# High and low activation parts interleaved by element in the gate stage of an encoder

## The chip, the cores and the metric

The kernel runs on one core of a Trainium2 chip. The metric is the time of one execution on the device, in microseconds (us). The engines are TensorE (PE in the profile; PEld is its loading of the stationary operand), VectorE (DVE), ScalarE (ACT), GpSimd (POOL) and SyncE (SP), which here only issues DMAs.

## What is computed

The reference is an encoder of two layers over 512 tokens of width 1024, batch 1, all in float32. Each layer adds a feed-forward, a mixer of four kinds of attention, a second feed-forward, and at its end a gated input:

```
for i in range(DEPTH):                      # DEPTH = 2
    x = x + 0.5 * swiglu(rms_norm(x, ffn1_norm[i]), ...)
    ...                                     # four attentions on x @ w_in, then w_out
    x = x + 0.5 * swiglu(rms_norm(x, ffn2_norm[i]), ...)
    gate = jax.nn.sigmoid(rms_norm(x, ple_norm[i]) @ ple_w_gate[i])
    x = x + gate * (p[i] @ ple_w_proj[i])
return rms_norm(x, final_norm)
```

Here `p[i]` is 512 x 256, `ple_w_proj[i]` 256 x 1024 and `ple_w_gate[i]` 1024 x 1024. The last two lines of the loop are the stage that the change touches; it is called the gate stage below.

## The kernel before

Activations lie transposed: a tile has 128 features on the partitions and the 512 tokens along the free dimension, and x is eight such tiles (`self.x`). [...] For an activation, `split` (L115) writes both into one tile of 128 x 2 x 512 words: ScalarE copies the source (with the gain of the norm as scale, L122, or without, L119) into `hl[:, 0]`, which rounds it, and VectorE writes the rest, source minus high part, into `hl[:, 1]` (L123 or L120). The 512 high words lie in a row and the 512 low words behind them. Weights come by DMA as float32 (`pieces`, L150) and are split the same way into `wh` (L173, ScalarE) and `wl` (L175, VectorE, or GpSimd in the mixer), a few pieces ahead of their use.

A product of a weight block and an activation tile is three matmuls into one PSUM tile, in `mm3y` (L195): high weight by high activation (L200), high by low (L201), low by high (L202). The weight block is the stationary operand (128 x 128), the activation part the moving one (128 x 512).

The orders of TensorE and of the DMA queue of SyncE are those of the program (`manual_schedule` in `run`, L846); the other engines are ordered by the framework's planner, and waits follow from which tiles an instruction reads and writes.

The gate stage goes so. While the second feed-forward writes its last results, `ple_in` (L827) loads the two tiles of p and splits them into `keep` tiles (`self.pin`). As each of the eight tiles of x is finished (L316, L317), `feed` (L251) splits x times the gain of the coming norm into a tile from `act()`, appended to `self.xn`, and `squared` adds to the sum of squares. `self.norm` holds the layer and the offset of that gain; G_PLE stands for the norm of the gate stage. `ple` (L793) then loops over 8 output tiles m: 6 matmuls for the projection of p (`pp`, with `pin`) and 24 for the gate (`gp`, with the eight tiles `xs`). At m = 0 the sum of squares is reduced (`rstat`, L221) and during m = 1 spread to all partitions (`rspread`, L239). `ple_out` (L818) scales the gate, takes a tanh, multiplies by `pp`, adds to x, and feeds the next stage. Two tags, "act" and "big", swap their roles after each layer (`self.tags.reverse()`), so in the rows the split tiles of x in the gate stage are named act in layer 0 and big in layer 1, and those of p keep. After layer 1 `final` (L837) scales the plain tiles that `feed` made in its other branch (L261) and stores them.

Of the kernel before, what the change touches and what calls it, by code (L numbers as in the profile page):

```python
# [29 lines left out]
G_FFN1, G_MIX, G_FFN2, G_PLE, G_GRP, G_Q, G_KV = 0, 8, 16, 24, 32, 40, 42  # L30
# [4 lines left out]
class Encoder:  # L35
# [215 lines left out]
    def feed(self, m, square=True):  # L251
        nc = self.nc
        l, off = self.norm
        t = self.act()
        if l < self.depth:
            self.split(t, self.x[m], self.g(l, off, m))
        else:
            self.squared(m)
            square = False
            t = t[:, 0].bitcast(F32)  # L260
            nc.scalar.activation(t, self.x[m], AF.Copy, scale=self.g(l, 0, m))  # L261
        self.xn.append(t)
        if square:
            self.squared(m)
# [562 lines left out]
    def ple_in(self, l):  # L827
        nc, a = self.nc, self.a
        self.pin = []
        for k in range(2):  # L830
            t = self.tmp()
            nc.sync.dma_start(t, a["p"][l, :, k])
            s = self.keep()
            self.split(s, t)
            self.pin.append(s)

# [8 lines left out]
    def run(self):  # L845
        with self.tc.manual_schedule(engines={mybir.EngineType.PE, mybir.EngineType.SP}):  # L846
            self.setup()
            self.begin(0, G_FFN1)
            for m in range(KC):
                self.feed(m, False)  # L850
                if m == 3:
                    self.prep()
            for l in range(self.depth):
                self.ffn(l, 0, (l, G_MIX))
                self.mix(l, (l, G_FFN2))
                self.ffn(l, 1, (l, G_PLE))
                self.ple(l, (l + 1, G_FFN1))
            self.final()


def grid(t, blocked=False):
# [118 lines left out]
```

## Time and profile before

| | us |
|---|---|
| Time before, median of 2 runs | 2167.8 |
| lowest and highest | 2166.63, 2168.96 |
| Span of the profiled execution | 2163.3 |
| TensorE matmuls busy in it | 2117.2 |
| VectorE busy | 1210.5 |
| ScalarE busy | 930.1 |
| GpSimd busy | 280.0 |

The profiled execution is one run, from its first instruction to its last. Its matmuls are pipelined: each is given as 0.39 us long, and the next one starts before it ends, so the pace of the stream is read from the starts, not from the lengths.

### The profile page before, as it was taken

Reading aid. Unit: us, or ns where it says so; the run is one execution under the profiler, and the core shown is the slowest. Engines: PE = TensorE matmul, PEld = TensorE weight load, DVE = VectorE, ACT = ScalarE, POOL = GpSimd, SP = SyncE. Lnnn points to the kernel's source line nnn. Section 1 sums busy time; section 2 is a strip of 40 time slices with the busy share of each in tenths; the row PEclk is TensorE's granted clock in tenths of the full one; section 3 lists DMA queues with packets and bytes.
Section 4 is the critical chain, followed back from the end, with each engine's and each line's share of the span. In section 5 each row is a group of like instructions: output and inputs, shape, how many; then the busy total and the mean of one; then the engine's idle time right before and its main releaser. Section 6 shows DMA issues by size and latency. Waiting matters only on the chain.

```text
span 2163.3 us, 25721 instructions
## 1 busy us (share of the span) xinstructions
PE 2117.2 (98%) x9564; PEld 1718.6 (79%) x9564; DVE 1210.5 (56%) x1926; ACT 930.1 (43%) x1690; POOL 280.0 (13%) x230
## 2 busy tenths in 40 slices
PE   8999999999999999999999999999999999999997
PEld 6888888677778888888888888886777788888886
DVE  5444446567766444456654444555687654444554
ACT  4332334477754332333533233345677533233343
POOL 2000001444321000001100000025332200000011
PEclk9999999999999999999999999999999999999998
DMA  3232223212112222223322322232121122322322
GB/s 129 97 109 99 98 94 111 90 60 75 40 54 93 98 96 99 98 98 96 100 96 98 94 102 98 93 102 93 64 59 49 59 98 98 94 101 98 102 92 89
DMA packets 63358, 195.38 MB, mean 90 GB/s; under 512 B 7552, under 2 KB 15872, under 8 KB 63232
## 3 DMA queue, kind: packets, MB, share of 16 engines
q1 hardware_dynamic: 61808, 187.92, 26.0%
q0 software_dynamic: 1280, 5.77, 1.0%
q8 instruction: 75, 1.23, 0.2%
q14 instruction: 51, 0.42, 0.1%
q10 hardware_dynamic: 144, 0.05, 0.0%
HBM read 189.51 MB, written 2.10 MB: 89 GB/s over the span
## 4 chain that ended last, share of the span: by engine, by line
PE 92%; DVE 4%; ACT 2%; issue 1%; DMA 1%; POOL 0%; POOLq 0%; SPq 0%; DVEq 0%; ACTq 0%
PE ps L200 15%; PE ps L201 15%; PE ps L202 15%; PE s L201 13%; PE s L200 13%; PE s L202 13%; PE pv L455 2%; PE s L439 2%; PE s L398 2%; PE s L397 1%; DVE kl L343 1%; PE s L225 1%; PE s L236 0%; ACT tmp L326 0%; DVE PT L443 0%
## 5 line engine op out<-in xcount | busy, mean ns | idle before, releaser
L173 ACT ACTIVATE wh<-raw 128x512 fp32r<-128x512 f32 (+1 forms) x712 | 437.8, 615 | 971.2 <-PE ps L201 457.3
L175 DVE TENSOR_TENSOR wl<-raw,wh 128x512 fp32r<-128x512 f32 (+1 forms) x614 | 435.6, 710 | 405.6 <-ACT wh L173 399.0
L200 PE MATMUL ps<-act,wh 128*128 128x512 f32 x616 | 248.8, 404 | 6.1 <-ACT act L122 6.1
L216 POOL TENSOR_TENSOR acc<-acc,tmp 128x512 f32<-128x512 f32 x54 | 72.3, 1340 | 1365.4 <-ACT tmp L215 1365.0
L200 PE MATMUL ps<-big,wh 128*128 128x512 f32 x616 | 247.0, 401 | 0.0
L201 PE MATMUL ps<-act,wh 128*128 128x512 f32 x616 | 242.7, 394 | 3.3 <-DVE act L123 3.1
L202 PE MATMUL ps<-act,wl 128*128 128x512 f32 x616 | 242.1, 393 | 0.0
L202 PE MATMUL ps<-big,wl 128*128 128x512 f32 x616 | 240.6, 391 | 0.0
L201 PE MATMUL ps<-big,wh 128*128 128x512 f32 x616 | 240.3, 390 | 0.0
L200 PE MATMUL s<-act,wh 128*128 128x512 f32 x520 | 202.4, 389 | 0.0
L200 PE MATMUL s<-big,wh 128*128 128x512 f32 x520 | 202.4, 389 | 0.0
L202 PE MATMUL s<-act,wl 128*128 128x512 f32 x520 | 202.3, 389 | 0.0
L202 PE MATMUL s<-big,wl 128*128 128x512 f32 x520 | 202.3, 389 | 0.0
L201 PE MATMUL s<-big,wh 128*128 128x512 f32 x520 | 202.3, 389 | 0.0
L201 PE MATMUL s<-act,wh 128*128 128x512 f32 x520 | 202.3, 389 | 0.0
L175 POOL TENSOR_TENSOR wl<-raw,wh 128x512 fp32r<-128x512 f32 (+1 forms) x98 | 127.4, 1300 | 286.6 <-ACT wh L173 286.4
L200 PEld LDWEIGHTS ps<-act,wh 128*128 128x128 f32 x616 | 116.7, 189 | 30.1 <-ACT act L122 6.4
L201 PEld LDWEIGHTS ps<-act,wh 128*128 128x128 f32 x616 | 116.7, 189 | 28.5 <-DVE act L123 7.3
L202 PEld LDWEIGHTS ps<-act,wl 128*128 128x128 f32 x616 | 116.6, 189 | 24.6
L202 PEld LDWEIGHTS ps<-big,wl 128*128 128x128 f32 x616 | 115.7, 188 | 24.7
L200 PEld LDWEIGHTS ps<-big,wh 128*128 128x128 f32 x616 | 116.0, 188 | 23.5 <-issue 1.1
L201 PEld LDWEIGHTS ps<-big,wh 128*128 128x128 f32 x616 | 116.2, 189 | 21.4
(172 smaller groups left out, 3373.1 us busy)
## 6 DMA issues: line engine op xcount, KB each, us to landing
raw<-in_ffn_gu SPq DMA_DIRECT2D x175, 512.0 KB, 3.5
raw<-in_ffn_d SPq DMA_DIRECT2D x64, 512.0 KB, 3.4
raw<-in_w_in SPq DMA_DIRECT2D x40, 512.0 KB, 3.5
raw<-in_ffn_d SPq DMA_DIRECT2D x64, 192.0 KB, 2.5
raw<-in_w_out SPq DMA_DIRECT2D x16, 512.0 KB, 3.5
raw<-in_ple SPq DMA_DIRECT2D x16, 384.0 KB, 3.0
raw<-in_ple SPq DMA_DIRECT2D x16, 256.0 KB, 2.6
nb<-in_na_bias POOLq DMA_DIRECT2D x8, 448.0 KB, 4.1
```

What stands on the lines that cost most here:

```text
L173: nc.scalar.activation(hi, r, AF.Copy)
L175: eng.tensor_tensor(out=lo, in0=r, in1=hi.bitcast(F32), op=ALU.subtract)
L200: nc.tensor.matmul(ps, lhsT=wh[:, k], rhs=x[:, 0], start=start and k == 0, stop=False)
L201: nc.tensor.matmul(ps, lhsT=wh[:, k], rhs=x[:, 1], start=False, stop=False)
L202: nc.tensor.matmul(ps, lhsT=wl[:, k], rhs=x[:, 0], start=False, stop=stop and k == last)
L216: eng.tensor_tensor(out=acc, in0=acc, in1=sq, op=ALU.add)
L225: nc.tensor.matmul(ss[:, t:t + 1], lhsT=acc[:, t * 128:(t + 1) * 128], rhs=self.ones, start=True, stop=True)
L343: nc.vector.tensor_tensor(out=kl[r], in0=u[r], in1=t[r, e].bitcast(F32), op=ALU.subtract)
L397: nc.tensor.matmul(s, lhsT=q[:, e, qs], rhs=k[0][:, e, k0:k1], start=True, stop=False)
L398: nc.tensor.matmul(s, lhsT=q[rows, e, qs], rhs=k[1][rows, k0:k1], start=False, stop=True)
L439: nc.tensor.transpose(tp[:, t * 128:(t + 1) * 128], h["P"][t][:, o:o + 128], self.ident)
L455: nc.tensor.matmul(pv[:, c], lhsT=vb, rhs=h["pt"][b][:, i, c], start=b == 0 and i == 0, stop=b == 3 and i == 1, skip_group_check=True)
```

## The change

The tiles that the gate stage's matmuls read as moving operands keep their size of 2 x 512 words for a partition, but are addressed so that high and low part of one element lie side by side: word 2t is the high part of token t, and word 2t + 1 its low part. `hl[:, 0]`, `hl[:, 1]`, `x[:, 0]` and `x[:, 1]` then stand for every second word. This holds for the eight tiles of the normed x of that stage (in `feed`, where the offset is that of its norm) and for the two tiles of p (in `ple_in`), in both layers. All other tiles, the weights, the instructions and their order in the program are as before.

```diff
@@ def feed @@
         t = self.act()
+        if off == G_PLE:
+            t = pairs(t)
         if l < self.depth:
             self.split(t, self.x[m], self.g(l, off, m))
@@ def ple_in @@
-            s = self.keep()
+            s = pairs(self.keep())
             self.split(s, t)
             self.pin.append(s)
@@ new function @@
+def pairs(t):
+    return t.rearrange("p a t -> p (a t)").rearrange("p (t a) -> p a t", a=2)
```

## Rows read from the trace of the kernel before

**Rows 1.** Head of the page: span, and busy time, share and instructions of each engine.
```profile
span 2163.3 us, 25721 instructions
PE 2117.2 (98%) x9564; PEld 1718.6 (79%) x9564; DVE 1210.5 (56%) x1926; ACT 930.1 (43%) x1690; POOL 280.0 (13%) x230
```

**Rows 2.** Page: the chain that ended last, share of the span by engine.
```profile
PE 92%; DVE 4%; ACT 2%; issue 1%; DMA 1%; POOL 0%; POOLq 0%; SPq 0%; DVEq 0%; ACTq 0%
```

**Rows 3.** Waits of TensorE, longest in total first: total us, times, longest us.
```profile
PE ps L200 <- ACT act L122: 6.1, 1, 6.1
PE s L368 <- DVE tmp L361: 6.0, 2, 3.0
PE s L397 <- DVE ne L404: 4.7, 4, 1.4
```

**Rows 4.** Windows over the gate stages of layers 0 and 1, busy us by engine.
```profile
core 0: us, PE busy (x) PEld busy (x) DVE busy (x) ACT busy (x) POOL busy (x), PEclk, DMA share, GB/s
1024.84:1080.66 55.82, 55.82 (x254) 46.33 (x252) 38.52 (x57) 27.64 (x48) 8.80 (x7) 1.00 0.32 97
2090.20:2145.86 55.66, 55.66 (x252) 45.98 (x251) 29.49 (x48) 26.23 (x46) 8.77 (x7) 1.00 0.26 78
```

**Rows 5.** Timeline of TensorE, gate stage of layer 0: start us, us, instruction.
```profile
1024.84 0.39 PE L200 MATMUL ps<-keep,wh 128*128 128x512 f32 x1
...
1026.20 0.39 PE L200 MATMUL s<-act,wh 128*128 128x512 f32 x1
...
1030.96 0.39 PE L200 MATMUL s<-act,wh 128*128 128x512 f32 x1
...
1080.66 0.39 PE L200 MATMUL ps<-big,wh 128*128 128x512 f32 x1
```

**Rows 6.** Timeline of TensorE, among the first matmuls of the kernel.
```profile
7.44 0.63 PE L202 MATMUL ps<-act,wl 128*128 128x512 f32 x1
7.87 0.63 PE L200 MATMUL ps<-act,wh 128*128 128x512 f32 x1
...
9.05 0.63 PE L202 MATMUL ps<-act,wl 128*128 128x512 f32 x1
9.47 0.62 PE L200 MATMUL ps<-act,wh 128*128 128x512 f32 x1
10.15 0.50 PE L201 MATMUL ps<-act,wh 128*128 128x512 f32 x1
```

**Rows 7.** Timelines of ScalarE and VectorE: split of the eighth tile, layers 0 and 1.
```profile
1026.83 0.73 ACT L122 ACTIVATE act<-x,gain 128x512 fp32r<-128x512 f32 x1 [1.43 <-DVE x L317]
1027.59 0.75 DVE L123 SCALAR_TENSOR_TENSOR act<-x,gain,act 128x512 fp32r<-128x512 f32 x1 [0.80 <-ACT act L122]
2092.79 0.75 DVE L123 SCALAR_TENSOR_TENSOR big<-x,gain,big 128x512 fp32r<-128x512 f32 x1 [0.80 <-ACT big L122]
```

**Rows 8.** Line 123 on VectorE: ns least/median/most, first and last start.
```profile
L123 DVE SCALAR_TENSOR_TENSOR act<-x,gain,act x32: 736/752/1832, 6.0 to 1027.6; 128x512 fp32r<-128x512 f32 x32
L123 DVE SCALAR_TENSOR_TENSOR big<-x,gain,big x32: 739/751/1835, 1044.3 to 2092.8; 128x512 fp32r<-128x512 f32 x32
```

**Rows 9.** Timeline of TensorE, first and last matmul of layer 1's gate stage.
```profile
2090.03 0.39 PE L200 MATMUL ps<-keep,wh 128*128 128x512 f32 x1
...
2145.63 0.39 PE L202 MATMUL s<-big,wl 128*128 128x512 f32 x1
```

**Rows 10.** Timelines: DMAs of p in layer 0, splits of p in layer 1.
```profile
953.23 0.86 SPq L832 DMA_DIRECT2D tmp<-in_p  x2
...
2031.78 1.90 DVE L120 TENSOR_TENSOR keep<-tmp,keep 128x512 fp32r<-128x512 f32 x3 [0.23 <-ACT keep L119]
```

## The prediction

> **What bounds the kernel now.** I read the head of the page first. The span is 2163.3 us, and TensorE's matmuls are busy for 2117.2 us of it, while VectorE has 56% and ScalarE 43% [rows 1]. A busy share of a pipelined engine proves little by itself, so the chain that ended last comes next: 92% of it is TensorE [rows 2]. Then the waits of TensorE: the longest is 6.1 us, at the start of the kernel, and the next is 6.0 us in two pieces [rows 3]. So the kernel is one stream of matmuls with hardly a hole, and a change counts by what it does to the spacing of matmuls.
>
> The change touches the gate stage that ends each layer. The stage of layer 0 lasts from 1024.84 to 1080.66 us, that of layer 1 from 2090.20 (a fifth of a microsecond after its first matmul) to 2145.86 us; TensorE is busy for all of both at a granted clock of 1.00, VectorE for 38.5 and 29.5 us and ScalarE for 27.6 and 26.2 us of some 55.7 [rows 4]. Spacing is read from starts, since the 0.39 us that one matmul lasts overlaps with the next: 21 matmuls lie between the starts 1026.20 and 1030.96, so 4.76 / 21 = 0.2267 us for 512 columns [rows 5]. [...]
>
> **The change, part by part.**
>
> *Matmuls with a step of two.* Each of the 8 output tiles takes 10 products (2 of the projection of p, 8 of the gate) of 3 matmuls: 30 x 8 = 240 in a layer, 480 in both. 240 x 0.2267 = 54.4 us, which is the stage but for its norm and transposes [rows 4, 5]. All 480 lie on the path that sets the end, one after another. The count stays the same; only the read of the moving operand changes, from 512 words in a row to every second of 1024. No row of this trace has a matmul, or any other instruction, that reads or writes with a step of two words, so the price is bounded:
> [...]
> - Nothing: the read has room to spare.
> - Twice the spacing: each fetch brings neighbouring words, and half of each is thrown away. Doubling 0.2267 gives +0.2267 x 480 = 108.8 us. The nearest rows with a spacing of about that size are the first matmuls of the kernel, 0.43 us (7.44 to 7.87) and 0.42 us (9.05 to 9.47) [rows 6]; they are slow for another reason than a step, but they are the same instruction shape. By 0.42 us the term is (0.42 - 0.2267) x 480 = 92.8 us.
> - Far end: the longest spacing in those rows is 0.68 us (9.47 to 10.15) [rows 6], +0.453 x 480 = 217.6 us.
>
> I take the doubled case, at the middle of its bounds: +0.21 us a matmul, 480 x 0.21 = 100.8 us. The reason is a comparison of rates: TensorE takes a word per partition every 0.2267 / 512 = 0.44 ns [rows 5], ScalarE's pass over 512 words lasts 0.73 us and VectorE's 0.75 us [rows 7], 1.4 and 1.5 ns a word. [...] If the memory hands out neighbouring words together, TensorE is the engine that lives on it. This is a choice and not a reading.
>
> [...]
>
> *Splits that write with a step of two.* In each layer 8 tiles of the normed x (ScalarE writes the high part, VectorE reads it and writes the low part) and 2 tiles of p: 20 pairs of instructions in all. Below, they cost what they cost now. Above, from the slowest row of that instruction, VectorE's goes from 0.75 to 1.83 us [rows 8], and ScalarE's doubles, from 0.73 to 1.46: 20 x 1.08 = 22 us and 20 x 0.73 = 15 us of busy time, beside engines that idle for 17 us or more of each stage [rows 4] and a matmul stream that would only be longer. The latest is the eighth tile of x: its low part ends at 1027.59 + 0.75 = 1028.34 [rows 7], and the first matmul on the tile starts at 1030.96 [rows 5], 2.6 us of cover; in layer 1 it is 2093.54 against 2096.15 (2090.03 + 27 x 0.2267) [rows 7, 9]. The upper bounds add 1.08 + 0.73 = 1.8 us, within it; without that cover each layer would pay what goes beyond 2.6 us. The tiles of p are issued at 953.23 for a first read at 1024.84, and split by 2033.68 for 2090.03 [rows 5, 9, 10]. I cost all this at nothing.
>
> *A wait that moves.* High and low parts now interleave, so their address ranges overlap. If dependencies go by ranges, the high matmul also waits for the low part. Queued behind it on TensorE is the whole stream, but the times just given are those of the low part, so the 2.6 us cover this too: nothing.
>
> *After the stage.* The next feed-forward's tiles and weights come no earlier; with TensorE slower, the others have more time. The tail after the last gate matmul (2145.63 to the span's end, 17.7 us [rows 9]) moves as a block; the last stage writes no interleaved tile for the final norm.
>
> **Sum.** 2163.3 + 100.8 = 2264.1 us of span; the median of the runs stands 4.5 us above the profiled span, so 2268.6 us.
>
> **Rivals.**
> [...]
> 2. *Partly hidden.* Fetches overlap in part, and the spacing lands half way to 0.43 us: (0.43 - 0.2267) / 2 x 480 = 48.8 us, 2217 us. [...]
> 3. *Worse than double.* The step lands on conflicts, or the clock drops as well: 0.68 us a matmul, 2168 + 218 = 2385 us. Nothing in these stages points to it: the clock is 1.00 in both [rows 4].
>
> **How the numbers follow.** Doubled 0.58, no change 0.28, partly hidden 0.09, worse 0.05. The forecast is that of the doubled case, 2268.6 us; its own range is 2258 to 2280 (92.8 to 108.8 us, and a little around it). As the rival without cost holds more than 2 in 10, the whole range reaches down to it and its gain, 2161, and up to 2285, for splits that are not wholly hidden. 2% of 2167.8 us are 43 us, about what a measurement of this kernel can tell from no change. Slower by more: the doubled and the worse case and most of the partly hidden one, 0.70. Within: the rival without cost and the rest, 0.29. Faster by 2%: 0.01, since the largest gain found is 6.4 us.
>
> **What would show it.** Right: in the timeline of the stage, starts of matmuls on interleaved tiles 0.42 to 0.45 us apart, matmuls of the other stages still at 0.227; each stage some 106 us long by the windows; VectorE and ScalarE with the same busy time in a stage nearly twice as long; no new wait of TensorE on a split. Wrong: a spacing of 0.227 in the stage (rival 1), 0.30 to 0.38 (rival 2), over 0.5 (rival 3), or a hole ahead of the first matmul on the eighth tile, which would make the splits the bound.

## The result and the profile after

The changed kernel takes 2274.2 us (two runs, 2273.68 and 2274.72) where the kernel before takes 2167.8: a ratio of 1.0489, 95% interval 1.0469 to 1.0508. The profiled execution spans 2271.9 us, 108.6 us more than before.

The head of its page and the chain that ended last, which answer to [rows 1, 2]:

```profile
span 2271.9 us, 25721 instructions
PE 2226.4 (98%) x9564; PEld 1730.5 (76%) x9564; DVE 1206.5 (53%) x1926; ACT 931.1 (41%) x1690; POOL 279.3 (12%) x230
...
PE 92%; DVE 4%; ACT 2%; issue 2%; DMA 1%; POOL 0%; SPq 0%; POOLq 0%; DVEq 0%; ACTq 0%
```

The instruction counts are the same on every engine. TensorE's busy time has grown by 109.2 us, about as much as the span; VectorE and ScalarE are where they were (1206.5 against 1210.5, 931.1 against 930.1). The shares of the chain look all but unchanged, and that is the trap of shares: nothing in them says that some matmuls became twice as slow.

The longest waits of TensorE in the changed kernel (total us, times, longest us), against [rows 3]:

```profile
PE s L370 <- DVE tmp L363: 6.0, 2, 3.0
PE ps L200 <- ACT act L122: 5.9, 1, 5.9
PE s L399 <- DVE ne L406: 4.6, 4, 1.4
```

The same three waits, each within 0.2 us of its length before (the diff moves line numbers beyond `feed` by two), and no new wait on a split among the longest. So the time is not in a hole. The windows over the two gate stages, columns as in [rows 4]:

```profile
core 0: us, PE busy (x) PEld busy (x) DVE busy (x) ACT busy (x) POOL busy (x), PEclk, DMA share, GB/s
1024.48:1134.14 109.66, 109.66 (x254) 51.91 (x252) 35.77 (x57) 28.00 (x49) 8.86 (x7) 0.98 0.18 54
2144.82:2254.46 109.64, 109.64 (x253) 51.62 (x251) 29.58 (x48) 26.65 (x46) 8.82 (x7) 0.98 0.13 40
```

The stages take 109.66 and 109.64 us, where they took 55.82 and 55.66: 107.8 of the 108.6 us are here. TensorE is busy throughout, before and after. The timeline of TensorE in the gate stage of layer 0 says how, the same four starts as in [rows 5]:

```profile
1024.48 0.61 PE L200 MATMUL ps<-keep,wh 128*128 128x512 f32 x1
...
1027.18 0.63 PE L200 MATMUL s<-act,wh 128*128 128x512 f32 x1
...
1036.69 0.63 PE L200 MATMUL s<-act,wh 128*128 128x512 f32 x1
...
1134.14 0.42 PE L200 MATMUL ps<-big,wh 128*128 128x512 f32 x1
```

21 matmuls in 9.51 us are 0.453 us each, twice the 0.2267 of before. Further on it is a little less: over the whole of both stages, without the starts next to the norm's small matmuls, the mean is 0.4515, against 0.2269 in the kernel before. 480 x (0.4515 - 0.2269) = 107.8 us, just what the two windows have grown by. The other 0.8 us of the span is not followed up; single runs of one kernel differ by more.

The split of the eighth tile, as in [rows 7]:

```profile
1026.47 0.75 ACT L122 ACTIVATE act<-x,gain 128x512 fp32r<-128x512 f32 x1 [1.44 <-DVE x L319]
1027.25 0.75 DVE L123 SCALAR_TENSOR_TENSOR act<-x,gain,act 128x512 fp32r<-128x512 f32 x1 [0.82 <-ACT act L122]
```

0.75 and 0.75 us, against 0.73 and 0.75. ScalarE's write with a step of two takes 0.02 us more, VectorE's read and write with it what they took, and the split ends 8.7 us before the first matmul on the tile (1036.69).

The granted clock of the stages is 0.98, not 1.00. In smaller windows it is one dip in each stage, shortly after the norm's single-column matmuls. Two windows of one microsecond in the dip of layer 0 (TensorE alone):

```profile
1041.00:1042.00 1.00, 1.00 (x3) 0.50 0.28 111
1042.00:1043.00 1.00, 1.00 (x3) 0.50 0.00 0
```

and the timeline of TensorE there:

```profile
1041.21 0.63 PE L202 MATMUL ps<-keep,wl 128*128 128x512 f32 x1
1041.66 0.63 PE L200 MATMUL s<-act,wh 128*128 128x512 f32 x1
1042.11 0.64 PE L201 MATMUL s<-act,wh 128*128 128x512 f32 x1
1042.57 0.64 PE L202 MATMUL s<-act,wl 128*128 128x512 f32 x1
1043.02 0.64 PE L200 MATMUL s<-act,wh 128*128 128x512 f32 x1
```

From 1041 to 1043 us the clock stands at 0.50, and the starts are 0.45 us apart, as they are at 1.00. Plain matmuls are slower there: where the kernel before has its clock at 0.50 (402 to 405 us), they start 0.43 us apart (403.45, 403.88, 404.31), against 0.2267 us at 1.00 [rows 4, 5]. The starts of the read with a step of two are as far apart at 0.50 as at 1.00, so it is not the granted clock that paces these matmuls.

### The profile page after: what moved, and what is told of

It is laid out like the page before. It is cut to its first block, busy times and chain, and to the rows that moved or that the text cites. A ratio compares the mean times of both kernels' runs of the same rounds, so it can differ in the third digit from the quotient of the medians.

```text
span 2271.9 us, 25721 instructions
## 1 busy us (share of the span) xinstructions
PE 2226.4 (98%) x9564; PEld 1730.5 (76%) x9564; DVE 1206.5 (53%) x1926; ACT 931.1 (41%) x1690; POOL 279.3 (12%) x230
## 4 chain that ended last, share of the span: by engine, by line
PE 92%; DVE 4%; ACT 2%; issue 2%; DMA 1%; POOL 0%; SPq 0%; POOLq 0%; DVEq 0%; ACTq 0%
PE ps L200 15%; PE ps L202 15%; PE ps L201 15%; PE s L200 13%; PE s L201 13%; PE s L202 13%; PE pv L457 2%; PE s L441 2%; PE s L400 1%; PE s L399 1%; PE s L225 1%; DVE kl L345 1%; PE s L236 0%; ACT tmp L328 0%; DVE PT L445 0%
## 5 line engine op out<-in xcount | busy, mean ns | idle before, releaser
L200 PE MATMUL s<-big,wh 128*128 128x512 f32 x520 | 217.9, 419 | 0.0
L200 PE MATMUL s<-act,wh 128*128 128x512 f32 x520 | 217.9, 419 | 0.0
L201 PE MATMUL s<-act,wh 128*128 128x512 f32 x520 | 217.9, 419 | 0.0
L201 PE MATMUL s<-big,wh 128*128 128x512 f32 x520 | 217.9, 419 | 0.0
L202 PE MATMUL s<-big,wl 128*128 128x512 f32 x520 | 217.9, 419 | 0.0
L202 PE MATMUL s<-act,wl 128*128 128x512 f32 x520 | 217.9, 419 | 0.0
```

Source lines behind the costliest of these rows:

```text
L200: nc.tensor.matmul(ps, lhsT=wh[:, k], rhs=x[:, 0], start=start and k == 0, stop=False)
L201: nc.tensor.matmul(ps, lhsT=wh[:, k], rhs=x[:, 1], start=False, stop=False)
L202: nc.tensor.matmul(ps, lhsT=wl[:, k], rhs=x[:, 0], start=False, stop=stop and k == last)
```

## The experiments

Which part of the change costs, how the price counts, and which reads are slow: twelve kernels, all built from the kernel before or the changed one. "Spacing" is the mean distance of starts of matmuls in the gate stage of layer 0; two rows of the timeline show it for each kernel, and "n between" says how many matmuls stand between them. Five kernels (a step of four; an odd start; repeated words; a step of two, each word twice; runs of four across the border) keep the splits of the kernel before and wrap each gate-stage tile in a small class: `self.t` is the tile, `i[1]` is 0 or 1 where the matmul asks for `x[:, 0]` or `x[:, 1]`, and the line returned is what it reads; the rest of the class is left out here. Those five, and the first two, mix up which words are multiplied; their arithmetic is not that of the reference.

**Only the writes.** The splits write interleaved, the matmuls read halves.

```diff
+        d = t
         if off == G_PLE:
             t = pairs(t)
...
-        self.xn.append(t)
+        self.xn.append(d if off == G_PLE else t)
...
-            s = pairs(self.keep())
-            self.split(s, t)
+            s = self.keep()
+            self.split(pairs(s), t)
```

> The splits still write high and low part interleaved (step of two), in the same 10 tiles of each layer, but the 480 matmuls read the first or the last 512 words of the tile in a row, which mixes high and low parts: the products are not those of the reference. If the read of the moving operand is the whole cost: spacing 0.227 us in the gate stage, 2168 us (within 4 us). If the writes of the splits, or the wait for both parts, carry the cost: near 2274 us.

Measured 2168.6 us, a ratio to before of 1.0007 (0.9997 to 1.0017). Timeline of TensorE, with six matmuls between the two rows:

```profile
1045.72 0.39 PE L202 MATMUL s<-act,wl 128*128 128x512 f32 x1
...
1047.31 0.39 PE L200 MATMUL s<-act,wh 128*128 128x512 f32 x1
```

1.59 / 7 = 0.227 us. The writes, and whatever wait comes with them, cost nothing that these runs can show.

**Only the reads.** The splits write halves, the matmuls read every second word.

```diff
-        self.xn.append(t)
+        self.xn.append(pairs(t) if off == G_PLE else t)
...
-            self.pin.append(s)
+            self.pin.append(pairs(s))
```

> The splits write high and low part each in a row, as before, but the 480 matmuls read every second word of the tile, which mixes high and low parts: the products are not those of the reference. If the read is the whole cost: spacing 0.453 us in the gate stage, 2274 us (within 4 us). If the writes carry it: 2168 us.

Measured 2275.1 us, ratio 1.0498 (1.0483 to 1.0514), the price of the full change. Timeline, five between:

```profile
1044.40 0.63 PE L200 MATMUL s<-act,wh 128*128 128x512 f32 x1
...
1047.10 0.63 PE L200 MATMUL s<-act,wh 128*128 128x512 f32 x1
```

2.70 / 6 = 0.45 us. How the words were written is of no account; the read alone carries the price.

**Only p.** The edit in `feed` is taken out again.

```diff
-        if off == G_PLE:
-            t = pairs(t)
```

> Only the two tiles of p are interleaved; the eight tiles of the normed x keep their halves. 96 of the 480 matmuls read with a step of two. If the price is one per matmul, 0.4525 - 0.2267 = 0.226 us each: 96 x 0.226 = 21.7 us, 2189 us. If part of it hung on the stage (the norm, the wait for the last split) and not on the count of matmuls, these 96, a fifth, would cost clearly more or less: all but nothing, or over 40 us.

Measured 2190.2 us against 2170.3 for the kernel before on that chip, +19.9 us; ratio 1.0088 (1.0071 to 1.0105), in which the 21.7 us expected lie (1.0100). Timeline at the seam from tiles of x to tiles of p:

```profile
1043.33 0.39 PE L201 MATMUL s<-act,wh 128*128 128x512 f32 x1
1043.56 0.39 PE L202 MATMUL s<-act,wl 128*128 128x512 f32 x1
1043.79 0.61 PE L200 MATMUL ps<-keep,wh 128*128 128x512 f32 x1
1044.22 0.63 PE L201 MATMUL ps<-keep,wh 128*128 128x512 f32 x1
1044.67 0.63 PE L202 MATMUL ps<-keep,wl 128*128 128x512 f32 x1
```

The distance goes from 0.23 to 0.45 us within one matmul or two and stays there as long as interleaved tiles are read. A price per matmul, nothing per stage.

**Runs of two.** My reason for the doubling had been that neighbouring words come together; how many, it had left open. If they come in pairs, pairs of neighbours should be enough.

```diff
-    return t.rearrange("p a t -> p (a t)").rearrange("p (t a) -> p a t", a=2)
+    return t.rearrange("p a t -> p (a t)").rearrange("p (t a r) -> p a t r", a=2, r=2)
```

(`split` gives its source the same shape.)

> Two high words, then two low words, and so on, written and read so; same values as before. Theory L (the moving operand is fetched in lines of four words, 0.4533 / 256 = 1.77 ns a line, whatever is wanted of it): each line still gives two wanted words, 256 lines, spacing 0.453 us, 2274 us. Theory W (fetched in pairs of neighbouring words, 0.89 ns a pair): 256 whole pairs, spacing 0.227 us, 2168 us. Theory S (any innermost step but one halves the rate): innermost step is one, 0.227 us, 2168 us.

Measured 2273.7 us, beside 2167.5 of the kernel before on that chip. Timeline, eleven between:

```profile
1056.15 0.63 PE L202 MATMUL s<-act,wh 128*128 128x512 f32 x1
...
1061.57 0.63 PE L202 MATMUL s<-act,wh 128*128 128x512 f32 x1
```

5.42 / 12 = 0.45 us: no better than single words. Pairs and "step other than one" both fall.

**A step of four.**

```diff
+        self.t = t.rearrange("p a t -> p (a t)").rearrange("p (t s) -> p s t", s=4)
...
+        return self.t[:, 2 * i[1]].unsqueeze(1).to_broadcast([128, 2, 256])
```

> Splits as before; each of the 480 matmuls reads 256 words with a step of four, twice over, in place of 512 in a row, so the products are not those of the reference. L: one wanted word a line, 512 lines at 1.77 ns, spacing 0.907 us, 480 x 0.68 = 326 us more than before, 2494 us. W: one wanted word a pair, as with a step of two, 0.453 us, 2277 us. S: 0.453 us, 2277 us.

Measured 2278.6 us. Timeline, five between:

```profile
1044.48 0.64 PE L202 MATMUL s<-act,wl 128*128 128x512 f32 x1
...
1047.24 0.64 PE L202 MATMUL s<-act,wl 128*128 128x512 f32 x1
```

2.76 / 6 = 0.46 us, where a fixed price for each line of four words had asked for 0.907. So the slow rate did not fall further: about a word per 0.9 ns, also where each word comes from four words of its own.

**Runs of four**, the same edit as for runs of two with `r=4`.

> Four high words, then four low words, and so on, written and read so; same values as before. A step of two, runs of two and a step of four all took 0.45 to 0.46 us, so theories L and W as first put have fallen. Theory Q (words go two at a time only out of whole groups of four words, 16 bytes, and otherwise one at a time): every group is whole, spacing 0.227 us, 2168 us. Theory R (any read that isn't one unbroken row goes one word at a time): 0.453 us, 2274 us.

Measured 2170.6 us, beside 2170.5 of the kernel before on that chip (one run each). Timeline, eleven between:

```profile
1044.12 0.39 PE L204 MATMUL s<-act,wl 128*128 128x512 f32 x1
...
1046.90 0.39 PE L204 MATMUL s<-act,wl 128*128 128x512 f32 x1
```

2.78 / 12 = 0.232 us. Four words in a row restore the rate; the 0.005 us left over would be 480 x 0.005 = 2.4 us, which one run cannot show in the time.

**Runs of 64**, with `r=64`.

> 64 high words, then 64 low words, and so on; same values as before. Q: 0.227 us, 2168 us. R: 0.453 us, 2274 us. If instead each of the 8 breaks in a row costs a little, the spacing shows it: 0.227 us plus 7 breaks.

Measured 2167.7 us, beside 2170.5. Timeline, nine between:

```profile
1049.68 0.39 PE L204 MATMUL s<-act,wl 128*128 128x512 f32 x1
...
1051.95 0.39 PE L202 MATMUL s<-act,wh 128*128 128x512 f32 x1
```

2.27 / 10 = 0.227 us: theory R falls, and breaks as such cost nothing.

**An odd start.**

```diff
+        self.t = t.rearrange("p a t -> p (a t)")
...
+        o = 510 * i[1] + 1
+        return self.t[:, o:o + 512]
```

> Splits as before, but the 480 matmuls read 512 words in a row that start one word (4 bytes) into the high part, or at the last word of it, so the products are not those of the reference. Q with groups that must start on 16 bytes: 0.453 us, 2274 us; Q with groups that may straddle: 0.227 to 0.24 us, 2168 to 2175 us. R: one unbroken row, 0.227 us, 2168 us.

Measured 2171.1 us, beside 2170.5. Timeline, twelve between:

```profile
1043.71 0.40 PE L200 MATMUL s<-act,wh 128*128 128x512 f32 x1
...
1046.77 0.39 PE L201 MATMUL s<-act,wh 128*128 128x512 f32 x1
```

3.06 / 13 = 0.235 us: a row that starts one word into the tile, or at word 511, loses 0.009 us in all, not half its rate.

**Repeated words.**

```diff
+        return self.t[:, i[1], 0:128].unsqueeze(2).to_broadcast([128, 128, 4])
```

> Splits as before, but each of the 480 matmuls reads 128 words in a row and takes each four times (innermost step zero), so the products are not those of the reference. [...] R: 0.453 us, 2274 us.

Measured 2161.7 us, beside 2170.5 (one run each). Timeline of the start of the gate stage, 28 between:

```profile
1024.79 0.38 PE L200 MATMUL ps<-keep,wh 128*128 128x512 f32 x1
...
1031.05 0.38 PE L202 MATMUL s<-act,wl 128*128 128x512 f32 x1
```

6.26 / 29 = 0.216 us. This spacing is 0.011 us below the 0.2267 of the kernel before, with the same instructions on a quarter of the words. So at least 0.011 us of every gate-stage matmul of the kernel before belong to its read. Over 480 matmuls they are 5 us; the rest of the 8.8 us between the two single runs is not explained by the spacing.

**A step of two, each word twice.**

```diff
+        return self.t[:, i[1], 0::2].unsqueeze(2).to_broadcast([128, 256, 2])
```

> Splits as before; each of the 480 matmuls reads 256 words with a step of two and takes each twice in a row (0, 0, 2, 2, 4, 4, ...), so the products are not those of the reference. Theory Q1 (the full rate needs four successive elements inside one stretch of 16 bytes, in whatever arrangement): words 0, 0, 2, 2 do, spacing 0.216 to 0.227 us, 2162 to 2168 us. Theory Q2 (they must be neighbours or equal, a gap of one word breaks it): 0.45 us, 2274 us.

Measured 2169.6 us, beside 2170.3 of the kernel before on that chip. Timeline, nine between:

```profile
1049.83 0.39 PE L202 MATMUL s<-act,wl 128*128 128x512 f32 x1
...
1052.09 0.39 PE L200 MATMUL s<-act,wh 128*128 128x512 f32 x1
```

2.26 / 10 = 0.226 us: a step of two at the full rate. The gap between words does no harm here, where four successive elements lie within four words; Q2 falls.

**Runs of four across the border.**

```diff
+        self.t = t.rearrange("p a t -> p (a t)").rearrange("p (t r) -> p t r", r=8)
...
+        return self.t[:, :, 2:6]
```

> Splits as before; each of the 480 matmuls reads words 2 to 5 of every eight, so that each run of four has two words on either side of a 16-byte border, and the products are not those of the reference. If whole stretches on 16-byte borders are fetched (two of which a run then touches, as with the runs of two): 0.45 us, 2274 us. If four neighbours are enough wherever they start: 0.227 to 0.24 us, 2168 to 2174 us, as with the odd start.

Measured 2273.3 us, beside 2170.3. Timeline, eleven between:

```profile
1058.20 0.63 PE L200 MATMUL s<-act,wh 128*128 128x512 f32 x1
...
1063.61 0.63 PE L200 MATMUL s<-act,wh 128*128 128x512 f32 x1
```

5.41 / 12 = 0.45 us. Four neighbours that start two words further on cost the double (0.45 against 0.232 us). What counts is where a run of four starts, reckoned in fours from the start of the tile: the border is at every fourth word.

**The weights instead.** The stationary operand of the gate stage is interleaved (in one tile for both parts, in all stages), the activations are not.

```diff
-                hi = self.tile("wh", [128, 512], F32R, 3)[:, :c]
-                lo = self.tile("wl", [128, 512], F32R, 3)[:, :c]
+                wt = self.tile("wh", [128, 2, 512], F32R, 3)
+                if src.tensor.name == "in_ple":
+                    wt = pairs(wt)
+                hi, lo = wt[:, 0, :c], wt[:, 1, :c]
```

> The weights of the gate stage, not the activations, have their high and low parts interleaved: LDWEIGHTS reads 128 words with a step of two, the moving operand is in a row. If the stationary operand falls to half rate too: 128 words at 0.88 ns in place of 0.44, 0.057 us more for a load of 0.188 us, 0.245 us, which no longer hides behind a matmul's 0.227: up to 480 x 0.018 = 9 us, 2177 us. If loads already go a word at a time: 0.188 us and 2168 us.

Measured 2178.3 us, against 2170.3. The group of weight loads in part of the gate stage (count, busy us, mean ns, idle), first of the kernel before:

```profile
L200 PEld LDWEIGHTS s<-act,wh 128*128 128x128 f32 x55 | 10.3, 188 | 2.1
```

and of this one:

```profile
L202 PEld LDWEIGHTS s<-act,wh 128*128 128x128 f32 x54 | 10.6, 197 | 2.0
```

and two rows of its timeline of TensorE, ten between:

```profile
1044.22 0.40 PE L202 MATMUL s<-act,wh 128*128 128x512 f32 x1
...
1046.82 0.40 PE L204 MATMUL s<-act,wh 128*128 128x512 f32 x1
```

The load takes 0.197 in place of 0.188 us, and the spacing is 2.60 / 11 = 0.236 us: 0.009 us each, 480 x 0.009 = 4.3 us. The load did not grow by the 0.057 us that the first reading asked for, so that reading is wrong, though its time, 2177 us, was all but met. Some half of the 8 us is from the interleaving. The rest is not settled. This kernel also has one common tile for both weight parts in all its stages, and outside the gate stages some waits of TensorE have grown, the one for `PT` in the attention from 1.9 to 7.0 us in total; that the common tile is the cause is not shown.

**What the reads have in common.** The words of a tile, taken in groups of four from its start, and how many of these groups a matmul goes through:

| read of 512 elements | groups visited | spacing, us |
|---|---|---|
| each word four times | 32 | 0.216 |
| a row; runs of 64 | 128 | 0.227 |
| step two, each word twice | 128 | 0.226 |
| runs of four | 128 | 0.232 |
| a row from an odd word | 129 | 0.235 |
| step two (the change); runs of two; fours across the border | 256 | 0.45 |
| step four | 512 | 0.46 |

0.2267 / 128 = 1.77 and 0.4515 / 256 = 1.76 ns a group. Up to two wanted words a group, TensorE gets one word per 0.9 ns; the full rate is there where each group visited gives four successive elements (three were not run). The 32 groups of the repeated words take 0.216 us and not a quarter of 0.227: what paces them is not shown. Besides them, only the step of four does not fit a price per group (0.9 ns for each of its 512): why a visit for one word is cheaper than one for two, the runs leave open.

## Why the prediction was right, and where it was off

*What bounds the kernel, and the count.* Right. 480 matmuls on the path that sets the end, no cover, and what their spacings have grown by is the change (107.8 of 108.6 us of span).

*The price of a matmul.* The doubling was right, the size off: I took +0.21 us, in the middle between a plain doubling (0.4533 us) and the first matmuls of the kernel (0.42). Measured is 0.4515, +0.225, all but the doubling itself; the term came to 107.8 us in place of 100.8. The step that failed is the lower bound from [rows 6]: those matmuls were slow for a reason of their own, as the prediction says itself, and a row of the right size is not a row of the same cause. The profiled span of 2271.9 lies 7.8 us above the sum; the time lies only 5.6 us above the 2268.6 forecast, because the median stands 2.3 us above the profiled span here and not 4.5. No run shows the gain of 6.4 us that the range reaches down to (2161): the change cost 106.4 us, and the shortest spacing of all runs, the 0.216 us of the repeated words, is 0.011 us below the kernel before, 5 us over 480 matmuls.

*The reason for the price.* Right in its size for this change, though it was a choice and not a reading, and not right as a rule. Neighbouring words do matter, and how many, which the prediction had left open, the runs give as four, reckoned from the start of the tile: runs of two were as slow as single words (0.45 us both), runs of four were at 0.232 us, and the same runs two words further on at 0.45. That half of each fetch is thrown away is not shown: a price per fetch, whatever is wanted of it, would have given the step of four 0.907 us, and it took 0.46; that part stays open.

*Splits, waits, what follows.* Right on all three: the writes alone are 1.0007 of before, ScalarE took 0.75 us (0.73 before) and VectorE 0.75 as before, and TensorE's longest waits are the same. Nothing was taken from the cover of 2.6 us; it grew to 8.7 us, since the slower stream reaches the eighth tile later.

*The rivals.* That the read has room to spare (0.28) fell with the spacing of 0.45 us. This step of two, and the runs of two, leave two wanted words in each group of four, and the rate is halved; the full rate was measured only where four successive elements came from a group (0.216 to 0.235 us). Partly hidden (0.09), which asked for 0.30 to 0.38 us, fell too. Worse than double (0.05) had the clock falling as well. It did fall, once in each stage for some 3 us, and cost next to nothing there: the starts are 0.45 us apart in the dip as outside it.

## What to carry to other kernels

How the words of a float32 moving operand lie decided TensorE's pace in these stages (0.2267 or 0.45 us for 512 words), while ScalarE and VectorE, three times slower per word (1.4 and 1.5 ns against 0.44), hardly noticed a step of two in the split of the eighth tile (0.75 us each, 0.73 and 0.75 before). Where two sequences must share a tile, interleave them by four words from its start (2170.6 beside 2170.5 us) or by 64 (2167.7), not by single words or pairs (+106 us for 480 matmuls). The step showed in no wait, no idle time and no share of the chain; look at the distance between starts.

## What the runs showed that I had not expected

- Two neighbouring words buy nothing over single ones (0.45 us both), and four neighbours lose the full rate when they start two words further on (0.45 against 0.232 us).
- A read that touches a quarter of the memory makes a matmul faster than in the gate stage of the kernel before: 0.216 against 0.2267 us. Each of those pays 0.011 us for its 512 different words.
- The granted clock fell to 0.50 in the middle of a stream without a hole (1041 to 1043 us in layer 0, 2160 to 2162 in layer 1), after the single-column matmuls of the norm (1038.06 and 2158.40), where at the same place of the kernel before it stayed at 1.00 [rows 4]. What differs in the rows is that TensorE's starts were 0.45 us apart before and after them, in place of 0.227. Over part of layer 0's stage the mean is below 1.00 in three more kernels whose x and p are read at the slow rate: 0.96 from 1030 to 1078 us with runs of two and with a step of four, 0.91 from 1040 to 1060 us with fours across the border. It is 1.00 from 1030 to 1078 and from 2100 to 2140 us with runs of four, runs of 64, the odd start and the repeated words, all read at the full rate. Why the clock falls is not shown.
